# Third and fourth value groups by seven products of quarters, and another order of heads, linear attention and gates

## The chip, the cores and the metric

The kernel runs on one core of a Trainium2 chip as a single launch. The metric is the device time of a launch in microseconds (us), lower is better. Five engines work side by side: PE (TensorE, matrix products), ACT (ScalarE), DVE (VectorE), POOL (GpSimd) and SP (SyncE, which here only issues transfers from HBM). PE's weight loads are listed apart as PEld.

## The reference, cut to what matters

Two layers, each a mixer of three groups behind one input projection `w_in`, a gate on each group, one output projection and a layer norm. SEQ is 256 and D_MODEL is 2048.

```python
def hybrid_layer(x, mem, w_in, ...):
    h = x @ w_in
    a_q, a_k, a_v, a_z, b_q, b_k, b_v, b_z, b_lr, m_q, m_z = jnp.split(h, cuts, axis=-1)
    y_a = chunk_band_attention(a_q, a_k, a_v, rel_table)       # 8 heads of 128
    log_g = jax.nn.log_sigmoid(b_lr @ gate_w + gate_b) / GATE_TAU
    o_b = gla_chunk_recurrence(b_q, b_k, b_v, log_g)           # gated linear attention, 4 heads
    o_b = o_b * lax.rsqrt(jnp.mean(jnp.square(o_b), axis=-1, keepdims=True) + RMS_EPS) * gla_norm_g
    mk, mv = jnp.split(mem @ w_mem_kv, 2, axis=-1)
    y_m = memory_attention(m_q, mk, mv)                        # 4 heads of 128, 256 memory tokens
    y = concat([y_a * silu(a_z), o_b * silu(b_z), y_m * silu(m_z)])
    return layer_norm(DEEPNORM_ALPHA * x + y @ w_out, ln_g, ln_b)
```

## The kernel before

**Numbers.** Every large product is made of float32r operands split in two: a number is its rounded high part plus a low part, and a product takes three matmuls (high·high, low·high, high·low).

**The stream of weights.** All weights lie in one list, `loads`, in the order in which PE uses them. SP fetches each one into a tile `raw` of a ring of four (`RAWS`), ACT rounds it to the high part `wh` (ring of four), DVE subtracts to get the low part `wl` (ring of three). `take()` hands PE the next weight and calls `advance()`, which makes the casts of the weight three places ahead (`HI_AHEAD`), the subtraction two places ahead (`LO_AHEAD`) and starts the transfers for which the ring has room. PE and SP execute in the order of the program text (`manual_schedule`); on ACT and DVE a scheduler sets the order, in which weight work comes with high priority.

**Pieces.** One weight's matmuls are a piece. There are three kinds. A wide piece W (`ws_pieces`, 512 KB) has weights as the stationary side and x as the moving one: 16 matmuls, 8 of 512 and 8 of 256 columns. Its output comes transposed, as heads and gates need it. A piece O (`as_pieces` with 512 columns, 512 KB) has x stationary: 12 matmuls of 512. A value piece (`as_pieces` with 388 columns, 388 KB) is 12 matmuls of 388.

**Values.** `asv` holds the 1552 columns that are wanted with tokens on partitions: b_lr (16), b_v (512) and a_v (1024), as four groups of 388 (`w388[l, 0..3]`). Groups 0 and 1 together are a product of 256 tokens by 776 columns, which is cut into 2 x 2 blocks and done by seven block products (Strassen's method in Winograd's form) for each quarter of the 2048 rows: three products use a weight block as it lies in HBM (`plain_products`: quarters B11, B22, B21), four use sums of weight blocks (`sum_products`). A block product is a `quarter()`, 6 matmuls of 388 columns. The sums are made by DVE: B11 and B12, B22 are fetched into the tiles `term` (three of them, one set for all quarters), `high(d)` adds a second term to the first in place (L260) and ACT and DVE then split the sum. The x side has its differences in `diff`. Groups 2 and 3 are plain: two runs of eight value pieces, `values(2)` and `values(3)`, with `values` copying the result to `asv`.

**The order of work.** A layer runs: memory keys and values; linear attention's q and k (G_BQK); wide pieces of heads 0 to 3 (G_AQ0, G_AK0) and 4 to 7 (G_AQ1) mixed with the narrow quarters by the strings `PART_B` (a W between two plain products) and `PART_A` (a W between two sums); then, with no mixing, `values(2)`, the rest of the wide ones, `values(3)`, G_AK1, G_MQ, G_BZ, G_AZ0, G_AZ1, G_MZ: eight pieces each, 64 in all. After that the output projection.

**The generators.** Linear attention (`gla`), attention heads (`a_head`), memory heads (`m_head`) and the norm's work are Python generators that are stepped by `tick()` after each piece; `yield n` lets n pieces pass before the next step. They are what stands between pieces in PE's order, and they hide their work on ACT and DVE behind the pieces that pass meanwhile. Heads run two at a time from the list `waiting`; `finish(gens)` ticks, with no pieces in between, until they are done. In a head: scores on PE, bias and maximum on DVE, Exp on ACT, `yield 1`, scaling on DVE, `yield 3`, transposes on PE (L742), a copy on ACT (L744), `yield 2`, the product with the values on PE, a copy on ACT (L751). `gla` begins with an identity transpose of b_lr and the gate logits, builds its intra-chunk scores level by level, and ends with: products into PSUM, four copies to two tiles `sc` on ACT (L686), their squares (L693), an inverse root (`rsqrt`, L509 on ACT), scaling on DVE (L699), and then a wait for the gate z (`gate`), which `put_gate` makes out of the pieces G_BZ with a Silu on ACT (L1137); two multiplications by z on DVE (L705), `yield 2`, eight transposes on PE (L711).

**After the heads.** A gate's piece group (G_AZ0, G_AZ1, G_MZ) multiplies a group of heads `yraw[i]` by a Silu; `split_y` and `differences` prepare y for the output projection, which uses seven products of quarters too, for `QUARTERS` of its rows.

## Time and profile before

| | value |
|---|---|
| time, median of 3 runs (lowest to highest) | 910.93 us (910.86 to 911.02) |
| the profiled execution | 910.88 us |
| its span in the trace | 909.1 us |
| granted PE clock, mean over the span | 0.998 of full speed |
| PE busy | 902.0 us, 99% |
| PEld busy | 792.9 us, 87% |
| DVE busy | 715.9 us, 79% |
| ACT busy | 550.4 us, 61% |
| POOL busy | 9.0 us, 1% |
| moved by DMA | 196.20 MB, mean 216 GB/s |
| weight transfers of 512 KB into `raw` | 254, 4.3 us to landing |
| weight transfers of 388 KB into `raw` | 64, 3.6 us to landing |
| transfers of 388 KB into `term` | 24, 4.2 us to landing |

Read it so: the profiled execution is as long as the median run, and the span leaves 1.78 us of it outside of the trace. PE is busy nearly all of the span, so its idle time is small and DVE is the engine with the next highest load. Busy time on PE is modelled from pipelined matmuls, so the duration of a piece is best taken as the difference of two starts.

### The profile page before, as it was taken

Reading aid. Unit: us, or ns where it says so; the run is one execution under the profiler, and the core shown is the slowest. Engines: PE = TensorE matmul, PEld = TensorE weight load, DVE = VectorE, ACT = ScalarE, POOL = GpSimd, SP = SyncE. Lnnn points to the kernel's source line nnn. Section 1 sums busy time; section 2 is a strip of 40 time slices with the busy share of each in tenths; the row PEclk is TensorE's granted clock in tenths of the full one; section 3 lists DMA queues with packets and bytes.
Section 4 is the critical chain, followed back from the end, with each engine's and each line's share of the span. In section 5 each row is a group of like instructions: output and inputs, shape, how many; then the busy total and the mean of one; then the engine's idle time right before and its main releaser. Section 6 shows DMA issues by size and latency. Waiting matters only on the chain.

```text
span 909.1 us, 14442 instructions
## 1 busy us (share of the span) xinstructions
PE 902.0 (99%) x5437; PEld 792.9 (87%) x5437; DVE 715.9 (79%) x990; ACT 550.4 (61%) x803; POOL 9.0 (1%) x24
## 2 busy tenths in 40 slices
PE   9999999999999999999999999999999999999997
PEld 7889999998888888888888899999988888888885
DVE  5697788698764877799989667886886769778996
ACT  5675655576575775655569555556756657665551
POOL 1000000000000000000000000000000000000000
PEclk9999999999999999999999999999999999999999
DMA  8868786775545457876776687666654565669752
GB/s 301 289 202 281 262 273 200 241 256 181 156 154 168 143 166 255 257 251 213 242 221 199 193 292 252 226 195 185 216 178 141 179 205 167 252 208 302 249 191 93
DMA packets 66997, 196.20 MB, mean 216 GB/s; under 512 B 7024, under 2 KB 9840, under 8 KB 66928
## 3 DMA queue, kind: packets, MB, share of 16 engines
q1 hardware_dynamic: 66544, 195.18, 65.6%
q8 instruction: 42, 0.69, 0.3%
q14 instruction: 27, 0.22, 0.1%
q0 software_dynamic: 384, 0.11, 0.1%
HBM read 193.16 MB, written 2.10 MB: 215 GB/s over the span
## 4 chain that ended last, share of the span: by engine, by line
PE 99%; DMA 0%; ACT 0%; SPq 0%; ACTq 0%; issue 0%
PE ps L86 97%; PE ps L742 1%; DMA raw<-w 0%; PE ps L840 0%; PE ps L780 0%; PE ps L711 0%; ACT res L887 0%; PE ps L608 0%; PE ps L543 0%; ACT wh L362 0%; SPq L355 0%; ACTq L1299 0%; ACT row L880 0%; PE ps L878 0%; PE ps L864 0%
## 5 line engine op out<-in xcount | busy, mean ns | idle before, releaser
L268 DVE TENSOR_TENSOR wl<-raw,wh 128x1024 fp32r<-128x1024 f32 (+1 forms) x313 | 364.8, 1168 | 123.8 <-PE ps L86 83.5
L261 ACT CAST wh<-raw 128x1024 fp32r<-128x1024 f32 (+1 forms) x313 | 314.2, 1008 | 230.8 <-PE ps L86 135.5
L86 PE MATMUL ps<-x,wh 128*128 128x512 f32 x1280 | 404.2, 397 | 0.0
L86 PEld LDWEIGHTS ps<-x,wl 128*128 128x128 f32 x1280 | 240.4, 188 | 56.6
L86 PE MATMUL ps<-wh,x 128*128 128x512 f32 (+2 forms) x984 | 286.8, 373 | 1.0 <-ACT wh L362 1.0
L86 PE MATMUL ps<-x,wl 128*128 128x256 f32 x1280 | 252.2, 278 | 0.0
L86 PEld LDWEIGHTS ps<-x,wh 128*128 128x128 f32 x1280 | 199.7, 189 | 1.6 <-issue 0.3
L86 PEld LDWEIGHTS ps<-wh,x 128*128 128x128 f32 x984 | 179.1, 188 | 24.6 <-ACT wh L362 1.3
L86 PE MATMUL ps<-wl,x 128*128 128x512 f32 (+2 forms) x492 | 182.6, 371 | 0.0
L86 PEld LDWEIGHTS ps<-wl,x 128*128 128x128 f32 x492 | 92.4, 188 | 12.6 <-DVE wl L363 0.2
L261 ACT CAST wh<-term 128x776 fp32r<-128x776 f32 (+1 forms) x39 | 36.0, 924 | 50.5 <-DVE term L260 42.8
L268 DVE TENSOR_TENSOR wl<-term,wh 128x776 fp32r<-128x776 f32 (+1 forms) x39 | 41.5, 1065 | 14.0 <-PE ps L86 13.5
L260 DVE TENSOR_TENSOR term<-term,term 128x776 f32<-128x776 f32 (+1 forms) x39 | 41.3, 1060 | 0.5 <-DMA term<-w 0.5
L86 PE MATMUL ps<-wh,s 128*128 128x512 f32 (+1 forms) x144 | 41.2, 367 | 0.0
L86 PEld LDWEIGHTS ps<-wh,s 128*128 128x128 f32 x144 | 25.8, 188 | 3.2
L86 PE MATMUL ps<-wl,s 128*128 128x512 f32 (+1 forms) x72 | 26.5, 368 | 0.0
L733 ACT ACTIVATE sc<-sc,mx 128x128 f32<-128x128 f32 (+1 forms) x32 | 14.2, 444 | 8.2 <-DVE mx L731 8.2
L86 PE MATMUL ps<-wh,sc 128*128 128x388 f32 x64 | 16.5, 338 | 0.0
L86 PEld LDWEIGHTS ps<-wl,s 128*128 128x128 f32 x72 | 13.5, 188 | 1.6
L504 DVE TENSOR_TENSOR s<-raw,s 128x512 fp32r<-128x512 f32 (+1 forms) x23 | 12.6, 569 | 2.3 <-ACT s L503 2.3
L500 DVE SCALAR_TENSOR_TENSOR sz<-ps,sz 128x512 f32<-128x512 f32 x20 | 13.6, 686 | 0.9
L86 PE MATMUL ps<-w,x 128*128 128x512 f32 (+1 forms) x72 | 14.3, 356 | 0.0
(226 smaller groups left out, 701.7 us busy)
## 6 DMA issues: line engine op xcount, KB each, us to landing
raw<-w SPq DMA_DIRECT2D x254, 512.0 KB, 4.3
raw<-w SPq DMA_DIRECT2D x64, 388.0 KB, 3.6
term<-w SPq DMA_DIRECT2D x24, 388.0 KB, 4.2
term<-w SPq DMA_DIRECT2D x15, 512.0 KB, 4.7
bias<-relw SPq DMA_DIRECT2D x16, 192.0 KB, 3.8
res<-xT SPq DMA_DIRECT2D x4, 512.0 KB, 6.3
res<-xn SPq DMA_DIRECT2D x4, 512.0 KB, 5.0
raw<-memT SPq DMA_DIRECT2D x4, 512.0 KB, 4.8
```

The source lines that it names most:

```text
L86: pe.matmul(o, l, r, start=start, stop=stop, skip_group_check=True)
L260: in_order(dve.tensor_tensor(d.raw, d.raw, d.plus, op=ALU.add))
L261: act.copy(d.hi, d.raw)
L268: in_order(dve.tensor_tensor(d.lo, d.raw, d.hi.bitcast(F32), op=ALU.subtract))
L500: dve.scalar_tensor_tensor(dst, a, scale, dst, op0=ALU.mult, op1=ALU.add)
L504: dve.tensor_tensor(lo, src, hi.bitcast(F32), op=ALU.subtract)
L733: act.activation(s[:, own[t]], s[:, own[t]], AF.Exp, bias=mx[:, t:t + 1], accum_out=zs[:, t:t + 1])
L742: pe.transpose(ps[:, pt, i * P:(i + 1) * P], s[:, i * P:(i + 1) * P], ident)
```

## The change

Groups 2 and 3 of the values are done like groups 0 and 1. `PART_B` and `PART_A` become `PART_V`, one pair of patterns for each pair of groups: `B` is a plain product of a quarter, `T` a product with a sum, `W` a wide piece. G_AK1 joins the mixed stream, which has 36 W and 56 narrow pieces before all heads start, and 40 pieces are left: G_MQ, G_AZ0, G_BZ, G_MZ, G_AZ1, eight each. All heads and the linear attention run within these. `values()` is gone. Yields are shortened in `gla` and the heads, a list `scored` takes the place of `finish()` ahead of `differences` (they need a tile of q and k to be free, and a head that has its scores has read them), and heads 4 to 7 come behind the memory heads.

```diff
-PART_B = "WB" * 12
-PART_A = "TW" * 16
+PART_V = (("WB" * 4 + "WBB" * 4, "TWTWTTW" * 4), ("BBBW" * 4, "TWTWTTW" * 4))
...
-            stream = iter([Load(w512[l, g, p], (4, 256)) for g in (G_BQK, G_AQ0, G_AK0, G_AQ1) for p in range(8)][4:])
...
-            loads.extend(next(stream if c == "W" else plain) for c in PART_B)
-            add_sums(b11, b12, b21, b22, 388, PART_A, dict(W=stream))
-            group(w388[l, 2], 2, 388)
-            loads.extend(stream)
-            group(w388[l, 3], 2, 388)
-            for g in (G_AK1, G_MQ, G_BZ, G_AZ0, G_AZ1, G_MZ):
+            stream = iter([Load(w512[l, g, p], (4, 256)) for g in (G_BQK, G_AQ0, G_AK0, G_AQ1, G_AK1) for p in range(8)][4:])
+            sums = []
+            for v, (plains, added) in enumerate(PART_V):
+                b11, b12, b21, b22 = ([w388[l, v * 2 + n, 2 * q + k] for q in range(4)] for k, n in ((0, 0), (0, 1), (1, 0), (1, 1)))
+                plain = iter([Load(b, (2, 388)) for b in b11 + b22 + b21])
+                loads.extend(next(stream if c == "W" else plain) for c in plains)
+                add_sums(b11, b12, b21, b22, 388, added, dict(W=stream), sums)
+            for g in (G_MQ, G_AZ0, G_BZ, G_MZ, G_AZ1):
...
     gla:
-        yield 3
+        yield 2
         dve.scalar_tensor_tensor(xx, xx, 0.0, na, op0=ALU.min, op1=ALU.subtract)
...
         ready = [(gkf, gqf), decayed(dd)]
-        yield 3
+        yield 2
...
-                yield 1
+                if v == 0:
+                    yield 1
...
     a_head:
+        scored.append(h)
...
             dve.tensor_scalar(s[:, own[t]], s[:, own[t]], zs[:, t:t + 1], None, op0=ALU.mult)
-        yield 3
+        yield 2
...
-        yield 2
+        yield 1 if h < 4 else 2
         po, = yield from banks(1)
...
         release(po)
-        yield 1
...
-        values(2)
         add_heads(0)
-        run(wide)
-        values(3)
-        run(heads())
-        add_heads(1)
-        q = [hd.tile([P, 4, T], F32R, name=nm("mq"), tag="qk", bufs=4) for _ in range(2)]
+        mq = operand()
+        q = [mq[:, :, 0], mq[:, :, 1]]
...
         memory[:] = gens[-1]
+        add_heads(1)
...
-        run(as_pieces(xq[l], 512, put_gate, True))
         for i in range(1, 4):
             def gate(j, a, b):
...
-                if i == 1 and j == 0:
+                if i == 2 and j == 0:
                     finish(gens[0])
                     split_y(0, 0)
                     split_y(0, 2)
...
-                    finish(gens[min(i + 1, 3)])
+                    while len(scored) < (8 if q else 4):
+                        tick()
...
             run(ws_pieces(l, gate, cut_y if i == 3 else None))
+            if i == 1:
+                run(as_pieces(xq[l], 512, put_gate, True))
```

What the program's order becomes in layer 0 is shown at three places. The changed file has other line numbers than those of the profile: L683, L690, L505, L696, L702 and L708 there are L686, L693, L509, L699, L705 and L711 here, and L731, L740, L257, L264, L1130 are L733, L742, L261, L268, L1137.

The first place is the end of the linear attention, on ACT. The tiles `sc_2550` and `sc_2551` (before) are its result, `ms` the sums of its squares, `z` the gate, `sc_..,mx_..` the scores of a head. Before, in two pieces that lie apart in the row, the squares and the root, and then the gate:

```order
L693 ACTIVATE sq_2553,ms_2552<-sc_2550 128x128 x4
L261 CAST wh_2637<-raw_2451 128x1024
L693 ACTIVATE sq_2553,ms_2552<-sc_2551 128x128 x4
L261 CAST wh_2664<-raw_2532 128x1024
L509 ACT_TABLE_LOAD
L509 ACTIVATE rs_u_416_2628<-ms_2552,eps 128x8
```

```order
L261 CAST wh_2917<-raw_2857 128x1024
L261 CAST wh_2941<-raw_2875 128x1024
L751 COPY yr_1683<-ps 128x256 x2
L261 CAST wh_2963<-raw_2903 128x1024
L1137 ACT_TABLE_LOAD
L1137 ACTIVATE z_2959<-ps 128x1024
```

After, on the same engine (the linear attention's result is now `sc_3130` and `sc_3131`, and heads 4 and 5 are `sc_3225` and `sc_3237`):

```order
L690 ACTIVATE sq_3133,ms_3132<-sc_3131 128x128
L505 ACT_TABLE_LOAD
L505 ACTIVATE rs_u_515_3212<-ms_3132,eps 128x8
L731 ACT_TABLE_LOAD
L731 ACTIVATE sc_3225,zs_3228<-sc_3225,mx_3227 128x128
L731 ACTIVATE sc_3225,zs_3228<-sc_3225,mx_3227 128x256
L731 ACTIVATE sc_3237,zs_3240<-sc_3237,mx_3239 128x128
L731 ACTIVATE sc_3237,zs_3240<-sc_3237,mx_3239 128x256
L257 CAST wh_3273<-raw_3116 128x1024
L1130 ACT_TABLE_LOAD
L1130 ACTIVATE z_3263<-ps 128x1024
L257 CAST wh_3295<-raw_3196 128x1024
```

Root, the Exps of two heads and the Silu of the gate have moved together, with three table loads; before, 27 rows lay between the root and the gate's table load.

The second place is what PE has there: the transposes of the linear attention's result. Before, they stand alone between two wide pieces:

```order
L86 MATMUL ps<-x_478,wh_2917 128x512 x2
L86 MATMUL ps<-x_478,wl_2943 128x256 x2
L711 MATMUL ps<-ident,sc_2550 128x128 x4
L711 MATMUL ps<-ident,sc_2551 128x128 x4
L86 MATMUL ps<-x_530,wh_2941 128x512 x2
```

After, the transposes of heads 4 and 5 stand right behind them:

```order
L86 MATMUL ps<-x_478,wh_3192 128x512 x2
L86 MATMUL ps<-x_478,wl_3247 128x256 x2
L708 MATMUL ps<-ident,sc_3130 128x128 x4
L708 MATMUL ps<-ident,sc_3131 128x128 x4
L740 MATMUL ps<-ident,sc_3225 128x128 x3
L740 MATMUL ps<-ident,sc_3237 128x128 x3
L86 MATMUL ps<-x_530,wh_3245 128x512 x2
```

Between the last products of the linear attention (`st,qb`) and these transposes there are now four pieces, the values' products of two memory heads and the scores of heads 4 and 5; before there were 16 pieces, with the transposes and products of heads 4 and 5, all of heads 6 and 7 and the scores of two memory heads.

The third place is SP's row of transfers where plain products are mixed with wide pieces. Before (128x776 is a 388 KB weight, 128x1024 one of 512 KB):

```order
L238 DMA raw_620<-w 128x1024
L238 DMA raw_626<-w 128x776
L238 DMA raw_664<-w 128x1024
L238 DMA raw_686<-w 128x776
L238 DMA raw_698<-w 128x1024
```

After, in the plain products of groups 2 and 3:

```order
L234 DMA raw_1362<-w 128x776
L234 DMA raw_1395<-w 128x776
L234 DMA raw_1428<-w 128x776
L234 DMA raw_1450<-w 128x1024
L234 DMA raw_1462<-w 128x776
L234 DMA raw_1480<-w 128x776
L234 DMA raw_1504<-w 128x776
L234 DMA raw_1516<-w 128x1024
```

Three narrow transfers now stand ahead of each wide one, in a ring of four.

More of the change, by code (lines that the diff above doesn't have):

```diff
@@ L166, in add_sums @@
                     loads.append(d)
-            def group(g, kp, n):
-                loads.extend(Load(g[i], (kp, n)) for i in range(16 // kp))
             for p in range(8):
@@ L1026, in hybrid_trunk_kernel @@
         asv = per.tile([P, 2, 1552], F32, name=nm("asv"), tag="asv")
-        bias = {}
-        def values(i):
-            run(as_pieces(xq[l], 388, lambda acc: act.copy(asv[:, :, i * 388:(i + 1) * 388], acc)))
+        bias, scored = {}, []
         def put_gla(i, a, b):
@@ L1041, in stream @@
             yield from ws_pieces(l, put_gla, None, 4)
-            for _ in range(3):
+            for _ in range(4):
                 yield from heads()
@@ L1115, in hybrid_trunk_kernel @@
             beside(others)
[L1116 removed]
+        gens.append([m_head(h, q, mk, mv, yraw[2][:, h]) for h in range(4)])
         waiting.extend(gens[-1])
         memory[:] = gens[-1]
+        add_heads(1)
         yq, ydiff = [], []
```

71 lines of the change are left out of this document (35 added, 36 removed).

## The prediction

> **What bounds the kernel now.** I read the page first (engines, chain), then PE's timeline in the mixed stage for the length of a piece, then groups by form for ACT and DVE, then the timelines at the two places where the new order lays small work close together. The page's rows of busy time, its chain, and three of its transfer rows:
>
> ```profile
> PE 902.0 (99%) x5437; PEld 792.9 (87%) x5437; DVE 715.9 (79%) x990; ACT 550.4 (61%) x803; POOL 9.0 (1%) x24
> ...
> PE 99%; DMA 0%; ACT 0%; SPq 0%; ACTq 0%; issue 0%
> ...
> raw<-w SPq DMA_DIRECT2D x254, 512.0 KB, 4.3
> raw<-w SPq DMA_DIRECT2D x64, 388.0 KB, 3.6
> term<-w SPq DMA_DIRECT2D x24, 388.0 KB, 4.2
> ```
>
> The chain is PE for 99%: nothing else is late now, so a removed matmul is worth its whole time, and every wait that the new order makes is paid in full. The execution took 910.88 us (span 909.1 and 1.78 around it), 0.05 under the median, so the sum is made against 910.9. A change under 0.2%, 1.8 us, is about what a measurement of this kernel can't tell from none.
>
> **What is removed.** PE's timeline in the mixed stage (start, us, ...):
>
> ```profile
> 100.16 0.62 PE L86 MATMUL ps<-x,wh 128*128 128x512 f32 x2
> ...
> 102.95 0.52 PE L86 MATMUL ps<-wh,x 128*128 128x388 f32 x2
> 103.30 0.34 PE L86 MATMUL ps<-wl,x 128*128 128x388 f32 x1
> 103.48 0.52 PE L86 MATMUL ps<-wh,x 128*128 128x388 f32 x2
> 103.83 0.34 PE L86 MATMUL ps<-wl,x 128*128 128x388 f32 x1
> 104.01 0.62 PE L86 MATMUL ps<-x,wh 128*128 128x512 f32 x2
> ```
>
> From 100.16 to 102.95 is a wide piece, 2.79 us; from 102.95 to 104.01 a quarter of six matmuls, 1.06, or 0.177 each. Groups 2 and 3 take 2 x 8 x 12 = 192 matmuls of 388 a layer, and 7 x 4 x 6 = 168 by quarters: 24 less a layer, 48 in all, 48 x 0.177 = **8.5 us**. Wide pieces are the same in number.
>
> **What is added off PE.** For each layer twelve more transfers into `term` (9.5 MB in all beside 196), 12 more adds into terms and 4 into `raw`, and 12 more casts and subtractions. Their prices, with those of a 512 KB weight, from the groups by form (xcount | busy, mean ns):
>
> ```profile
> L268 DVE TENSOR_TENSOR wl<-raw,wh 128x1024 fp32r<-128x1024 f32 x249 | 303.7, 1221 | 91.1 <-PE ps L86 59.7 <-issue 12.4 <-ACT wh L261 9.0
> L268 DVE TENSOR_TENSOR wl<-term,wh 128x776 fp32r<-128x776 f32 x24 | 23.2, 967 | 11.9 <-PE ps L86 11.7
> L260 DVE TENSOR_TENSOR term<-term,term 128x776 f32<-128x776 f32 x24 | 23.0, 959 | 0.0
> L261 ACT CAST wh<-raw 128x1024 fp32r<-128x1024 f32 x249 | 260.8, 1051 | 186.0 <-PE ps L86 115.2 <-DMA raw<-w 41.4 <-issue 13.9
> ```
>
> On DVE that is 32 adds by 0.96 and 24 subtractions by 0.97, 54 us, and 12 combinations more; 716 becomes some 780 of 910. It lies beside PE's products. In a row `TWTWTTW`, PE has 4 x 1.06 + 3 x 2.79 = 12.6 us of work and DVE 4 x (0.96 + 0.97) + 3 x 1.22 = 11.4 at most. These two windows show that DVE can be this full (columns: window, length, PE, PEld, DVE, ACT, POOL, clock, DMA share, GB/s), the second with the cover nearly gone:
>
> ```profile
> 109.40:171.50 62.10, 62.10 (x357) 56.52 (x356) 51.84 (x59) 31.87 (x37) 0.00 (x0) 1.00 0.72 232
> 366.80:455.40 88.60, 88.60 (x392) 73.23 (x391) 81.43 (x83) 50.21 (x51) 0.00 (x0) 1.00 0.74 243
> ```
>
> PE lost nothing with DVE at 92%. I cost it at nothing. Four more table loads on ACT count only at the two places below.
>
> **The ring.** In `BBBW` a wide weight always meets the same one of four `raw` tiles. That tile's cycle is landing 4.3, cast 1.05, subtraction 1.22 and some 0.2 to issue (my estimate from the gaps between these rows), 6.8 us; PE needs 3 x 1.06 + 2.79 = 5.97 for the four pieces. Four rounds lose at most 4 x 0.8 = 3.3 us, out of a stock of three weights cast ahead, which is worth three narrow pieces (3.2) or more. The nearest stage of before, one narrow to one wide with the first terms:
>
> ```profile
> 84.00:98.00 14.00, 14.00 (x82) 12.73 (x81) 7.99 (x8) 7.12 (x9) 0.00 (x0) 1.00 0.85 297
> ```
>
> 297 GB/s without a wait of PE; `BBBW` asks (3 x 0.397 + 0.524 MB) / 5.97 us = 288. Between no loss and 3.3 us a layer I take 0.3, near the row without a loss: **0.6 us**.
>
> **Heads 0 and 1.** The gates' logits, and behind them the copies of the heads' transposes, are rows of one queue on ACT. Before, the same work (first a row of PE, last the copies' mean from the groups):
>
> ```profile
> 256.13 0.82 PE L742 MATMUL ps<-ident,sc 128*128 128x128 f32 x6
> ...
> 176.88 0.83 ACT L554 ACTIVATE sc<-ps,gb 128x256 f32<-128x256 f32 x2
> ...
> 179.28 0.63 ACT L558 ACTIVATE sc<-sc 128x512 f32<-128x512 f32 x1
> 179.92 1.28 ACT L559 ACT_TABLE_LOAD   x1
> 181.22 0.63 ACT L559 ACTIVATE sc<-sc 128x512 f32<-128x512 f32 x1
> ...
> L744 ACT COPY sc<-ps 128x384 f32<-128x384 f32 x16 | 6.8, 478 | 0.0
> ```
>
> From the end of the logits' products, PE has a wide piece, the six transposes (0.82, of which the modelled end overlaps the next row; some 0.6) and another wide piece before it wants the first copy: 2.79 + 0.6 + 2.79 = 6.2. In the new order a weight's cast and a scaling of 512 columns (0.63, as L558) come on ACT ahead of L559's table load, and that cast's `wh` is free only when the first wide piece ends, at 2.79: 2.79 + 1.05 + 0.63 + 1.30 + 0.63 + 0.48 = 6.9 for the first copy, 7.4 for the second, which is wanted at 6.6. At the least, with the cast free at once, there is no wait (the same sum begins 1.3 earlier, behind L554 and DVE's L557); at the most 0.8. I take 0.7 a layer, since the ring of `wh` is full in this stage: **1.4 us**.
>
> **The end of the linear attention.** This is the main cost. PE's rows there, before:
>
> ```profile
> 241.45 1.58 PE L86 MATMUL ps<-qk,qk 128*128 128x128 f32 x8
> 242.68 0.58 PE L86 MATMUL ps<-x,wh 128*128 128x512 f32 x1
> ...
> 247.64 0.74 PE L86 MATMUL ps<-x,wh 128*128 128x512 f32 x2
> ...
> 311.58 1.53 PE L86 MATMUL ps<-sc,mv 128*128 128x256 f32 x12
> 312.96 0.63 PE L86 MATMUL ps<-x,wh 128*128 128x512 f32 x2
> ```
>
> Count from the end of `st,qb` (247.64 before). In the new order PE has two memory heads' products (312.96 - 311.58 = 1.38), two heads' scores (242.68 - 241.45 = 1.23) and four pieces (11.16): it wants the transposes at 13.8. ACT and DVE, before:
>
> ```profile
> 247.31 2.39 ACT L686 COPY sc<-ps 64x512 f32<-64x512 f32 x4
> ...
> 254.02 1.04 ACT L261 CAST wh<-raw 128x1024 fp32r<-128x1024 f32 x1
> 255.08 1.28 ACT L509 ACT_TABLE_LOAD   x1
> 256.37 0.30 ACT L509 ACTIVATE rs_u<-ms,eps 128x8 f32<-128x8 f32 x1
> 259.21 1.29 DVE L699 TENSOR_TENSOR sc<-sc,rr 128x512 f32<-128x512 f32 x2
> 292.70 1.28 ACT L1137 ACT_TABLE_LOAD   x1
> 294.00 1.03 ACT L1137 ACTIVATE z<-ps 128x1024 f32<-128x1024 f32 x1
> ...
> L733 ACT ACTIVATE sc<-sc,mx 128x128 f32<-128x128 f32 (+1 forms) x32 | 14.2, 444 | 8.2 <-DVE mx L731 8.2
> L751 ACT COPY yr<-ps 128x256 f32<-128x256 f32 x16 | 5.7, 367 | 1.3 <-PE ps L86 1.3
> ```
>
> The first copy starts at -0.3. From it to the table load were 255.08 - 247.31 = 7.77 with two casts; now one cast less and two copies of 0.37 more, 7.5. Then in ACT's row: load and root 1.6, load 1.3, four Exps 4 x 0.44 = 1.8, cast 1.04, load 1.3, Silu 1.03. z is there at -0.3 + 7.5 + 8.1 = 15.2. DVE multiplies the first half by it (1.29 / 2 = 0.65), subtracts a weight (1.22), multiplies the second half (0.65): 17.7. PE has done the first four transposes in the meantime and stands from 14.3 to 17.7: 3.4 us a layer, **6.8 us**. Before, the same transposes came 47 us after the copies and waited for nothing. What could shorten it: nothing on ACT in that row can start earlier than the one ahead of it, but squares that overlap a little, and a subtraction that falls in another gap, could take 0.5 to 1.2; what could lengthen it is a late cast.
>
> The Trainium skill ("ScalarE: Activation LUTs", section "What ACT_TABLE_LOAD costs") puts a switch of tables at about 2.7 us with the drain of the engine. The rows show otherwise: the cast ends at 255.06, the load starts at 255.08 and the root at 256.37, 1.3 us in all.
>
> **The sum.** 910.9 - 8.5 + 0.6 + 1.4 + 6.8 = 911.2. Taking 0.2 a layer off the end's wait, for the overlaps just named, I say **910.8**: no change that can be told.
>
> **The rivals.**
> *The waits are half or less (faster).* For it: every wait is a difference of two long sums; if ACT's row at the end runs 1.7 us shorter and the head's copies come in time, 910.8 - 3.4 - 1.4 = 906.0, and with no waits at all 902.4. Against it: the order of ACT is fixed, and its rows have measured lengths. Center 905.5.
> *The ring (slower).* If landing in `BBBW` is 4.3 or more throughout and the stock gives only 1 us, each layer loses 2.3: 910.8 - 0.6 + 4.6 = 914.8. It decides from a landing above 5.97 - 1.05 - 1.22 - 0.2 = 3.5 us for 512 KB. For it: the median is 4.3; the first terms of the next sums go out in the same stage. Against: 297 GB/s without a wait.
> *PE's clock (slower).* These rows show what the clock does (the clock stands ahead of the DMA share):
>
> ```profile
> 903.00:905.00 2.00, 1.13 (x6) 0.64 (x4) 1.11 (x2) 1.67 (x4) 0.00 (x0) 1.00 0.52 188
> 905.00:907.00 2.00, 0.00 (x0) 0.00 (x0) 0.00 (x0) 0.01 (x1) 0.00 (x0) 0.58 0.92 330
> ```
>
> With PE idle for 2 us the granted clock is 0.58, with gaps 1.00. If the piece behind the long wait ran at 0.58, it would take 2.79 / 0.58 = 4.8, 2.0 more a layer: 914.8. The Trainium skill ("TensorE: Matmul & The Clock Gate", "Part 1: The HAM clock gate") has the clock halve after an idle window of 3.4 us that runs freely; by that rule a wait of this length would seldom fill a window, and these rows neither show nor exclude it.
> *Loads twice as dear (slower).* If a load held ACT for two times 1.28 where functions alternate, the three at the end add 3.8 a layer: 918.5. No row speaks for it.
>
> **How the numbers follow.** No change by the sum 0.44, waits half or less 0.31, ring 0.16, clock 0.07, loads 0.02. The first case's own range is 908.3 to 913.3, and it gives 0.07 to faster, 0.32 to no change, 0.05 to slower. So faster 0.38, the same 0.32, slower 0.30. The range 904.5 to 914.8 leaves out the lower part of the second case, half of the third and fourth and the last.
>
> **What would show it.** In the changed trace: 48 fewer matmuls of 388 on PE; a gap of about 3.4 us in PE ahead of the transposes L708, with the multiplication L702 named as its releaser, twice; about 0.6 us ahead of the first product with values; PE without gaps in `BBBW`. I am wrong if z's Silu ends well before 15 us after `st,qb`, if gaps with a `raw` transfer as their releaser come up among the narrow pieces, or if DVE's subtractions are late in the forty pieces.

## The result, and the profile after

The changed kernel takes 937.62 us (937.25 to 937.87) against 910.89 us of the kernel before beside it: 1.0294 times as long (95% interval 1.0276 to 1.0312). It is 26.7 us slower; 910.8 was forecast, in a range up to 914.8. With the 8.5 us of matmuls that are gone, 35 us of waits are to be found. In one of the runs below, that of the banks' order, one execution of four took 2425.81 us; it is left out of that run's time.

The page of the changed kernel, its engines, its chain and its weight transfers:

```profile
span 935.6 us, 14558 instructions
...
PE 905.8 (97%) x5389; PEld 785.5 (84%) x5389; DVE 769.6 (82%) x1058; ACT 573.2 (61%) x833; POOL 8.9 (1%) x24
...
PE 80%; DVE 8%; DMA 5%; ACT 4%; issue 3%; SPq 0%; ACTq 0%; DVEq 0%
...
raw<-w SPq DMA_DIRECT2D x254, 512.0 KB, 4.5
raw<-w SPq DMA_DIRECT2D x64, 388.0 KB, 4.3
term<-w SPq DMA_DIRECT2D x48, 388.0 KB, 4.1
```

The 48 matmuls are gone (5437 to 5389). The chain, 99% PE before, has 20% of other engines, and a value weight now lands in 4.3 us, not 3.6.

Where it went, by windows (window, length, PE, PEld, DVE, ACT, POOL, clock, DMA share, GB/s). Each goes from a layer's first value product to the first product with a sum in its output projection. Before:

```profile
64.41:373.63 309.22, 309.22 (x2033) 278.17 (x2032) 233.94 (x342) 193.32 (x302) 3.23 (x7) 1.00 0.65 211
511.72:819.40 307.68, 307.68 (x2026) 276.83 (x2025) 234.00 (x336) 190.65 (x293) 1.62 (x4) 1.00 0.64 208
```

After, each of the two in two parts, the mixed stream and the forty pieces (with the first pieces of the output):

```profile
64.06:230.84 166.78, 162.74 (x914) 146.23 (x913) 138.63 (x158) 91.86 (x112) 0.00 (x0) 1.00 0.74 253
230.84:382.80 151.96, 146.89 (x1098) 126.92 (x1096) 122.16 (x219) 112.39 (x205) 3.22 (x7) 1.00 0.55 182
521.38:684.51 163.13, 160.89 (x914) 146.72 (x913) 133.44 (x144) 90.39 (x108) 0.64 (x2) 1.00 0.76 255
684.51:845.31 160.80, 148.44 (x1091) 127.45 (x1088) 127.41 (x227) 111.66 (x201) 0.98 (x2) 0.99 0.53 170
```

Layer 0 takes 318.74, 9.5 more than before, layer 1 323.93, 16.3 more: together 25.8 of the 26.7. Since 4.25 us of matmuls are gone in each, layer 0 has 13.8 us of waits and layer 1 has 20.5. A stream is 36 x 2.79 + 56 x 1.06 = 159.8 us of pieces: 7.0 us of the waits of layer 0 lie there and 3.3 of layer 1. The forty pieces have the rest, 6.8 and 17.2. (PE busy is modelled; the differences of starts show more waits than the idle time.)

**In the stream.** The stage `BBBW`, in layer 0 and 1:

```profile
153.00:177.00 24.00, 21.75 (x120) 18.95 (x119) 16.03 (x19) 12.82 (x17) 0.00 (x0) 1.00 0.87 294
606.00:630.00 24.00, 21.76 (x120) 19.21 (x119) 16.19 (x18) 13.13 (x17) 0.00 (x0) 1.00 0.86 289
```

PE is without work for 2.2 us in each, 3.4 and 3.3 by the starts of its matmuls, while DVE is busy for two thirds and ACT for half: a weight is late. By the starts, nearly all of it falls into the third of the four rounds, which takes 9.28 us in both layers; the others take 5.97 to 6.06. What SP issued from 155 to 162 us landed late, and from 159 on the DMA engines had no time left:

```profile
raw<-w SPq DMA_DIRECT2D x4, 388.0 KB, 6.8
term<-w SPq DMA_DIRECT2D x3, 388.0 KB, 6.6
raw<-w SPq DMA_DIRECT2D x1, 512.0 KB, 6.8
...
159.00:162.00 3.00, 3.00 (x19) 2.53 (x18) 1.91 (x2) 0.91 (x2) 0.00 (x0) 1.00 1.02 347
162.00:165.00 3.00, 2.12 (x12) 1.57 (x10) 0.49 (x1) 1.23 (x2) 0.00 (x0) 1.00 1.01 393
```

The three terms in between, 1.2 MB, are those of the first sums. Layer 0 loses 3.4 more from 85 to 110 us, in the first plain products. In the stages of the sums, where DVE has most to do, PE waits for nothing:

```profile
177.00:230.80 53.80, 53.80 (x310) 49.13 (x309) 47.89 (x53) 29.55 (x34) 0.00 (x0) 1.00 0.70 242
630.00:684.50 54.50, 54.50 (x314) 49.74 (x313) 48.67 (x54) 29.87 (x36) 0.64 (x2) 1.00 0.71 242
```

**At the first transposes.** PE's and DVE's rows (start, us; in brackets the idle time before and what ended it):

```profile
230.84 0.38 PE L539 MATMUL ps<-ident,asv 128*16 128x128 f32 x2
232.19 0.55 DVE L471 TENSOR_TENSOR asv<-asv,ps 128x388 f32<-128x388 f32 x1
232.84 0.30 PE L860 MATMUL ps<-ident,lng 128*128 128x128 f32 x1 [1.61 <-issue]
```

The next matmul begins when DVE's last combination, L471, has read its PSUM bank: 1.8 us here, 1.7 in layer 1.

**At the end of the linear attention.** ACT, DVE and PE:

```profile
326.26 1.28 ACT L1130 ACT_TABLE_LOAD   x1
327.56 1.03 ACT L1130 ACTIVATE z<-ps 128x1024 f32<-128x1024 f32 x1
...
328.62 0.69 DVE L702 TENSOR_TENSOR sc<-sc,z 128x512 f32<-128x512 f32 x1 [0.41 <-ACT z L1130]
329.23 1.22 DVE L264 TENSOR_TENSOR wl<-raw,wh 128x1024 fp32r<-128x1024 f32 x1
330.36 0.69 DVE L702 TENSOR_TENSOR sc<-sc,z 128x512 f32<-128x512 f32 x1
...
329.37 0.66 PE L708 MATMUL ps<-ident,sc 128*128 128x128 f32 x4 [0.60 <-DVE sc L702]
331.20 0.63 PE L708 MATMUL ps<-ident,sc 128*128 128x128 f32 x4 [1.17 <-DVE sc L702]
```

2.1 us by the starts, and the same in layer 1.

**In layer 1 alone.** DVE and PE:

```profile
719.33 2.08 DVE L855 TENSOR_TENSOR res<-res,sc 128x512 f32<-128x512 f32 x3 [2.35 <-DMA sc<-ln_g]
...
725.42 1.69 PE L86 MATMUL ps<-mk,x 128*128 128x256 f32 x12 [1.64 <-DVE pairs L636]
...
758.16 0.69 PE L86 MATMUL ps<-sc,sc 64*64 64x64 f32 x32 [3.26 <-DVE sc L583]
...
815.33 1.07 PE L740 MATMUL ps<-ident,sc 128*128 128x128 f32 x6 [2.13 <-DVE sc L735]
```

Three waits for DVE that layer 0 has not or has shorter. L855 is the norm of the residual (`norm_residual`), sixteen operations of 0.69 us that run only in layer 1, among the forty pieces. DVE also stands still for the rows that they multiply by, 9.2 us in four places:

```profile
DVE res L855 <- DMA sc<-ln_g: 9.2, 4, 3.6
```

**The clock.** Three windows of 5 us, the first with PE idle for 3 us:

```profile
755.00:760.00 5.00, 1.84 (x37) 1.60 (x38) 5.00 (x13) 4.97 (x13) 0.00 (x0) 1.00 0.51 183
770.00:775.00 5.00, 3.34 (x56) 2.41 (x54) 4.23 (x11) 3.06 (x5) 0.00 (x0) 0.87 0.17 66
775.00:780.00 5.00, 5.00 (x24) 4.44 (x24) 2.02 (x4) 2.82 (x15) 0.00 (x0) 0.79 0.47 144
```

The clock falls in the linear attention's last products, where the matmuls are small and PE is without work for 1.6 us in all: 5 x 0.13 + 5 x 0.21 = 1.7 us lost. Behind the longest wait (758) it does not. The trace has the clock at half from 773.73 to 777.15 us, for 3.41 us. Windows of that length on the same grid, two around the wait that ends at 758, the one ahead of the halved one, and it:

```profile
753.25:756.67 3.42, 1.65 (x37) 1.08 (x35) 3.42 (x7) 3.39 (x6) 0.00 (x0) 1.00 0.46 148
756.67:760.08 3.41, 1.92 (x38) 1.64 (x39) 3.41 (x10) 3.38 (x11) 0.00 (x0) 1.00 0.43 159
770.32:773.73 3.41, 1.79 (x39) 1.31 (x42) 3.31 (x9) 1.52 (x3) 0.00 (x0) 1.00 0.16 61
773.73:777.15 3.42, 3.42 (x31) 3.09 (x24) 2.91 (x5) 1.58 (x5) 0.00 (x0) 0.50 0.43 114
```

The wait of 3.3 us lies across the border of two windows and leaves PE about half busy in each; the small matmuls and their waits lie in one, which is half busy too. The last section counts what follows such windows.

### The profile page after: what moved, and what is told of

Its sections match the earlier page's. It is cut to its first block, busy times and chain, and to the rows that moved or that the text cites. A ratio compares the mean times of both kernels' runs of the same rounds, so it can differ in the third digit from the quotient of the medians.

```text
span 935.6 us, 14558 instructions
## 1 busy us (share of the span) xinstructions
PE 905.8 (97%) x5389; PEld 785.5 (84%) x5389; DVE 769.6 (82%) x1058; ACT 573.2 (61%) x833; POOL 8.9 (1%) x24
## 4 chain that ended last, share of the span: by engine, by line
PE 80%; DVE 8%; DMA 5%; ACT 4%; issue 3%; SPq 0%; ACTq 0%; DVEq 0%
PE ps L86 78%; DVE wl L264 4%; DMA raw<-w 2%; DMA sc<-ln_g 1%; ACT wh L257 1%; DMA sc<-ln_b 1%; PE ps L740 0%; DMA lm<-lmask 0%; DVE res L855 0%; DVE mx L763 0%; PE ps L836 0%; DVE sc L583 0%; DVE sc L582 0%; DVE sc L574 0%; ACT sc L731 0%
## 5 line engine op out<-in xcount | busy, mean ns | idle before, releaser
L264 DVE TENSOR_TENSOR wl<-raw,wh 128x1024 fp32r<-128x1024 f32 (+1 forms) x313 | 364.5, 1169 | 94.3 <-PE ps L86 44.9
L257 ACT CAST wh<-raw 128x1024 fp32r<-128x1024 f32 (+1 forms) x313 | 313.0, 1007 | 203.7 <-PE ps L86 91.9
L86 PE MATMUL ps<-wh,x 128*128 128x512 f32 (+2 forms) x824 | 245.5, 379 | 0.0
L86 PEld LDWEIGHTS ps<-wh,x 128*128 128x128 f32 x824 | 150.4, 188 | 24.2 <-ACT wh L358 0.4
L86 PE MATMUL ps<-wl,x 128*128 128x512 f32 (+2 forms) x412 | 155.7, 378 | 0.0
L257 ACT CAST wh<-term 128x776 fp32r<-128x776 f32 (+1 forms) x63 | 56.3, 893 | 81.2 <-DVE term L256 64.8
L264 DVE TENSOR_TENSOR wl<-term,wh 128x776 fp32r<-128x776 f32 (+1 forms) x63 | 64.6, 1026 | 7.6 <-PE ps L86 6.8
L256 DVE TENSOR_TENSOR term<-term,term 128x776 f32<-128x776 f32 (+1 forms) x63 | 64.5, 1023 | 6.7 <-DMA term<-w 6.4
L86 PE MATMUL ps<-wh,s 128*128 128x388 f32 (+1 forms) x208 | 58.3, 362 | 1.8 <-ACT wh L257 1.8
L86 PE MATMUL ps<-wl,s 128*128 128x388 f32 (+1 forms) x104 | 37.9, 364 | 0.8 <-DVE wl L264 0.8
L86 PE MATMUL ps<-wl,sc 128*128 128x388 f32 x64 | 21.7, 339 | 0.3 <-DVE wl L264 0.3
L86 PEld LDWEIGHTS ps<-wh,sc 128*128 128x128 f32 x128 | 21.5, 189 | 0.0
L256 DVE TENSOR_TENSOR raw<-raw,term 128x776 f32<-128x776 f32 (+1 forms) x21 | 21.4, 1021 | 0.0
L855 DVE TENSOR_TENSOR res<-res,sc 128x512 f32<-128x512 f32 x16 | 10.6, 689 | 9.7 <-DMA sc<-ln_g 9.2
```

What stands on the lines that cost most here:

```text
L86: pe.matmul(o, l, r, start=start, stop=stop, skip_group_check=True)
L256: in_order(dve.tensor_tensor(d.raw, d.raw, d.plus, op=ALU.add))
L257: act.copy(d.hi, d.raw)
L264: in_order(dve.tensor_tensor(d.lo, d.raw, d.hi.bitcast(F32), op=ALU.subtract))
L855: dve.tensor_tensor(r, r, row, op=op)
```

## The experiments

The diffs are against the changed kernel if nothing else is said. Times are medians; the kernel before took 910.86 to 911.24 beside all of them.

**The order alone.** Groups 2 and 3 are plain pieces again, in the stream.

```diff
-("BBBW" * 4, "TWTWTTW" * 4))
+("BW" * 16, ""))
...
+        def values():
+            for i in (2, 3):
+                yield from as_pieces(xq[l], 388, lambda acc: act.copy(asv[:, :, i * 388:(i + 1) * 388], acc), at=i * 2)
...
-            narrow = plain_products(l, asv, n1, n2)
+            narrow = plain_products(l, asv, n1, n2) if v == 0 else values()
```

> Groups 2 and 3 as plain value pieces (16 of 12 matmuls, one wide piece behind each), all else as in the changed kernel: the new order alone. 8.5 us of matmuls come back. The trace of the changed kernel has some 13.5 us of PE waits in the mixed stream (layer 0: 3.3 in the first plain products, 3.4 in the second ones, 1.8 at the first transposes; layer 1: 3.3 and 1.7) and some 21 in the forty pieces. Theory 'both': the stream's waits go, but for those of the first plain products, and the forty pieces' stay: 937.6 + 8.5 - 10.2 = 936. Theory 'products' (the whole loss comes with the seven products): about 911. Theory 'order' (the whole loss is the forty pieces'): 937.6 + 8.5 = 946.

943.45 us, ratio 1.0356 (1.0340 to 1.0371). With the new order alone the kernel loses 32.4 us; with the products it loses 5.8 less, their 8.5 and what this run has of waits of its own, less the waits that they make. The gap at the first transposes is not there (0.2 us from one start to the next): without products there are no combinations. The forty pieces' waits are all there. My 936 was too low: I had counted on the stream's waits to go, and 2.6 us a layer of others came in `BWBW` (for DVE's combinations of the first pair of groups, by the rows that ended them), and 5.1 us of halved clock against 1.7. Without the two (5.2 and 3.4 us), 24 us remain to the order.

**The sums' terms later.**

```diff
-                ahead = FIRST_SUM_AHEAD if
+                ahead = 5 if d.sum[0] == 4 else FIRST_SUM_AHEAD if
```

> The first terms of groups 2 and 3 are fetched five weights ahead and not ten, so that they don't go out in the middle of the plain products BBBW. If it is their 1.2 MB in one go that makes the ring's transfers land in 7 us there, the 3.3 us a layer of waits go: 937.6 - 6.7 = 931. If the ring of four itself is too short for three narrow weights to one wide one, the waits stay: 937 to 938. If the terms now come too late for the first sum, it gets slower: 938 to 942.

939.36 us (1.0294 to 1.0325). The waits of the stage are 3.0 and 2.8 us by the starts, where they were 3.4 and 3.3. But the terms have not left the stage: in layer 0 they are issued from 162.1 to 166.5 us and not from 155.5 to 158.0, and the slow round is now the fourth (8.50 us; the third has 6.46). The DMA engines are full there, and not before:

```profile
159.00:162.00 3.00, 3.00 (x19) 2.65 (x18) 2.07 (x3) 1.56 (x2) 0.00 (x0) 1.00 0.86 250
168.00:171.00 3.00, 2.82 (x16) 2.40 (x15) 0.97 (x1) 1.33 (x3) 0.00 (x0) 1.00 1.00 388
171.00:174.00 3.00, 2.05 (x8) 1.31 (x8) 2.46 (x3) 2.06 (x3) 0.00 (x0) 1.00 0.99 381
```

In layer 1 it is the same, 8.12 us in the fourth round. The waits went where the terms went; a run with the terms outside of the stage was not made.

**Five raw tiles.** The room is that of the biases, which now lie in the third term's tile.

```diff
-HI_AHEAD, LO_AHEAD, RAWS = 3, 2, 4
+HI_AHEAD, LO_AHEAD, RAWS = 3, 2, 5
...
-            bias[h] = hd.tile([P, 384], F32, name=nm("bias"), tag="bias", bufs=3)
+            bias[h] = pairs_of_bias[:, h % 2, :384]
```

> Five raw tiles in place of four; the room comes from the biases of the heads, which now lie two at a time in the third term's tile and are fetched when the score before has read its own. If the ring is too short for BBBW (a tile's cycle of 6.8 us and more, four tiles, one weight each 1.7 us, where PE takes one each 1.49), the waits of 3.3 us a layer go, and with them part of those of layer 0's first plain products: 937.6 - 6.7 to 10 = 928 to 931. If the DMA engines are what is short there, they stay: 936 to 938. Biases that come late would cost 0 to 2 us, in the forty pieces.

934.97 us (1.0228 to 1.0271). The same two windows:

```profile
153.00:177.00 24.00, 22.69 (x127) 20.27 (x126) 17.34 (x18) 14.34 (x18) 0.00 (x0) 1.00 0.77 269
606.00:630.00 24.00, 23.54 (x133) 21.28 (x133) 18.43 (x19) 14.45 (x19) 0.00 (x0) 1.00 0.80 278
```

PE idles 1.3 and 0.5 us there, for 2.2 and 2.2, and by the starts the waits of the stage fall from 6.7 to 3.1 and those of layer 0's first plain products from 3.4 to 1.1. So a longer ring takes away half of the stage's waits and most of the others (the first plain products wait for 0.4 to 1.1 us in all four profiles with five tiles). It does not clear the DMA engines: their mean share is lower (0.77 and 0.80), but in layer 0 they are full again from 156 to 162 us (1.00 and 1.01), behind the terms, and the waits that are left follow at once. The terms make the transfers late, and the ring's length sets how much of that PE feels. The total won 2.6 of these 5.9 us, for this profile lost 6.8 us to the halved clock and the changed kernel's 1.7.

**Two wide pieces to three narrow ones.**

```diff
-("BBBW" * 4, "TWTWTTW" * 4))
+("BWBBW" * 4, "TWTWTT" * 4))
```

> The plain products of groups 2 and 3 as BWBBW and the sums as TWTWTT: four wide pieces a layer go from the sums to the plain products, three narrow weights to two wide ones instead of three to one. The ring waits 3.3 us a layer in BBBW; fetching the terms later did not change this. If the stage is short of time for its transfers (the DMA engines are busy 0.87 of it, the highest share of any), they go, 937.6 - 6.7, and the sums pay where VectorE has 4 x 1.76 + 2 x 1.13 = 9.3 us of work to 9.8 of PE: 0 to 2 us a layer. So 931 to 935. If the waits have another reason: 937 to 942.

948.85 us (1.0402 to 1.0433), outside of all that was expected. `BWBBW` waits for 0.3 us at most, which a short ring and a shortage of transfer time would both have, but the sums now wait: 3.4 and 4.0 us among the last rows of them and 3.5 at the first transposes, in each layer. Rows of the sums with 9.8 us of PE for 9.3 of DVE are too tight. Besides, this profile loses 10.2 us to the halved clock.

**The combinations' priority, their banks, the sums' adds, and one piece more.** Four edits on the gap at the first transposes (shortened, and in part in words):

```diff
 e5:  c12, c21, c22 = asv[:, 0, n2], asv[:, 1, n1], asv[:, 1, n2]
+     with tc.high_priority(AHEAD) around the six combinations
 e11:
-            if d.plus is not None:
+            if d.plus is not None and (d.shape[1] == 512 or d.sum[0] < 4):
 e16: the heads and the linear attention are added behind the first piece of G_MQ
+        queries = ws_pieces(l, put_mq)
+        run(queries, 1)
+        beside(gens[0] + others)
+        add_heads(0)
+        run(queries)
 e18:
-        free[:] = [4, 5, 6, 7]
+        free[:] = [6, 7, 4, 5]
```

> The combinations of the third and fourth group's products (L466 to L471) get the high priority on VectorE that weight work has. The first PE work after the stream (the scores of heads 0 and 1) writes the four PSUM banks that these combinations read, and in the changed kernel it begins 1.8 us late in each layer, when the last combination ends. If this is the reason, both gaps go and nothing else: 937.6 - 3.5 = 934. If weights are then late by the 3.3 us of combinations, it is given back: 937 to 938.

> Leaves out the sums of the weights for groups 2 and 3 (sixteen adds of 0.96 us on VectorE a layer; the casts and subtractions stay). If VectorE's arrears at the end of the sums make the gap of 1.8 us at the first transposes, where a higher priority of the combinations changed nothing, both gaps go: 937.6 - 3.5 = 934. If they come from the order of the last piece alone: 937 to 938.

> Linear attention and heads start one wide piece later, so that two pieces (5.6 us more one: 8.4) and not 5.6 us lie between the last sum and the first work on the combinations' PSUM banks; VectorE has 7.6 us of combinations, subtractions and a total there. If that sum is the reason for the gaps of 1.8 us at the first transposes: -3.5, 934; the forty pieces have one piece less behind, which may cost up to 2.8 at the end of the heads. If it is a wait for something else, the gaps stay: 937 to 940.

> One line: after the stream the free PSUM banks are given out in the order 6, 7, 4, 5. The combinations read 6 and 7 first and 5 last; the first transposes and scores now take 6 and 7. If the gap of 1.8 us a layer at the first transposes is the wait for the bank that the last combination reads, most of it goes: 937.6 - 2.5 to 3.5 = 934 to 935. If VectorE's row itself is what the heads wait for (their scores' scaling stands behind the combinations), the wait moves to the transposes of heads 0 and 1: 937 to 938.

The priority: 937.57 us (1.0277 to 1.0307), the gaps as before, 1.8 and 1.7. Without the adds: 939.35 us (1.0293 to 1.0326), the gaps as before; DVE even stood idle for 1.8 us ahead of the last subtractions, so it isn't in arrears. One piece later: the gaps are gone, and the time is 945.24 us (1.0357 to 1.0396). The banks: the gap is 1.0 in layer 0 and gone in layer 1, and the time is 939.60 us (1.0301 to 1.0342). So the gap is the wait for the bank that the last combination reads, on account of what DVE has to do behind the last sum, and it stands in no relation to DVE's load before. That neither cure makes the kernel faster has two reasons that the profiles show. One piece later, the wait at the linear attention's end is 6.7 us a layer, with a piece of its cover gone:

```profile
801.69 1.94 PE L708 MATMUL ps<-ident,sc 128*128 128x128 f32 x8 [6.50 <-DVE sc L702]
803.42 1.49 PE L740 MATMUL ps<-ident,sc 128*128 128x128 f32 x6
804.56 1.20 PE L86 MATMUL ps<-x,wh 128*128 128x512 f32 x2
805.56 0.63 PE L86 MATMUL ps<-x,wl 128*128 128x256 f32 x2
```

And behind such a wait PE runs at half its clock: a pair of matmuls of 512 columns took 1.20 us, where 0.63 is usual. Windows of 5 us there:

```profile
795.00:800.00 5.00, 0.19 (x2) 0.00 (x0) 4.03 (x13) 3.70 (x10) 0.00 (x0) 0.98 0.20 59
800.00:805.00 5.00, 3.31 (x15) 3.34 (x16) 3.44 (x5) 2.02 (x4) 0.00 (x0) 0.50 0.87 215
805.00:810.00 5.00, 5.00 (x25) 4.28 (x25) 4.42 (x9) 2.44 (x7) 0.11 (x1) 0.84 0.61 251
```

0.1 + 2.5 + 0.8 = 3.4 us lost; over the whole profile 10.2, and in that of the banks' order 5.1.

**The mask later.** The two operations that wait for a transfer go behind the sums.

```diff
-                dve.tensor_copy(lmask, lm)
-                dve.tensor_tensor(eye, ident[:, :CH], ident[:, CH:], op=ALU.add)
             for c in added:
                 run(wide if c == "W" else narrow, 1)
+            if l == v == 0:
+                dve.tensor_copy(lmask, lm)
+                dve.tensor_tensor(eye, ident[:, :CH], ident[:, CH:], op=ALU.add)
```

> In layer 0, VectorE's two operations on the transferred mask and identity (L1064, L1065) stand behind the sums of the first groups instead of ahead of them. In the trace VectorE stands 1.2 us for these transfers, and PE has 3.3 us of gaps from 85 to 110 us, which layer 1 doesn't have. If the standing makes those behind 98 us: 937.6 - 2 to 2.4 = 935.4. If it is the x differences that share this stage: 937 to 938.

939.06 us (1.0291 to 1.0321). The waits from 85 to 110 us are 2.3 and not 3.4 us. That shows nothing of the mask: in the other profiles with four tiles, which all leave it in its place, the same waits are 1.8 to 3.9 us, and with the rows fetched ahead, an edit of layer 1, they are 2.2. In the total a gain of that size can't be told, where this profile lost 6.8 us to the clock.

**The residual's norm: rows fetched ahead, left out, left out before, in other places.**

```diff
 e3:
+            for row, a in zip(fetched, (ln_g, ln_b)):
+                sp.dma_start(row, a[l:l + 1, columns(n)].to_broadcast([P, 512]))
+            yield 4
 e4, e12 (of the kernel before):
-            others = [norm_residual(l - 1)]
+            others = [iter([1])]
 e10:
                 run(as_pieces(xq[l], 512, put_gate, True))
+                if l:
+                    beside(others)
 e15:
         for c in OUT_B[l]:
             run(sequences[c], 1)
+        finish([arrears])
```

> The norm's gain and offset rows of layer 1 (L852) are fetched four pieces before VectorE multiplies by them, and not just ahead. In the trace VectorE stands 9.2 us for these transfers in layer 1's forty pieces with the weights' and the heads' work queued behind. If this standing makes layer 1's waits there (some 15 us against 5.5 in layer 0), most of the difference goes: 937.6 - 7 to 9.5 = 928 to 931. If it is the sixteen multiplications themselves (11 us of VectorE), little goes: 936 to 938.

> Leaves out the normalisation of the residual in layer 1 (sixteen VectorE operations and eight transfers). If these are why layer 1 waits longer than layer 0 in its forty pieces: 937.6 - 10 = 927.6. If layer 1 waits for another reason: 936 to 938. The difference to the kernel with the rows fetched ahead is the price of the operations themselves.

> The kernel before, with the normalisation of the residual left out in layer 1 as above. If its place among 64 pieces covered it wholly: 910.9, no change. If it cost there too: 905 to 909, and the loss by the new order is smaller than 8.6 by that.

> The normalisation of the residual in layer 1 starts behind G_BZ, in the last sixteen pieces, with yields of 3 for 6; nothing is left out. Leaving it out took 8.6 us off. If it is only in the wrong place, all of that comes: 929. If its sixteen operations need the cover of the whole stage, wherever they stand, it waits in the gates instead: 934 to 938.

> The residual's norm of layer 1 in the first ten pieces of the output projection, behind all heads and gates, with yields of 2. Nothing is left out. If only the forty pieces lack cover for it, it is as good as leaving it out: 929. If VectorE and the fetch of its rows delay the output's weights: 931 to 936.

Rows ahead: 938.18 us (1.0287 to 1.0322), nothing won. But the edit did not do what it was for. The rows land when they did (719.22 us the first, for 719.31), DVE's operations begin as they land, and DVE stands for them almost as long, 8.0 us for 9.2:

```profile
DVE res L857 <- DMA sc<-ln_g: 8.0, 4, 3.6
```

So this run does not say what the standing costs. Left out: 929.04 us (1.0186 to 1.0224), 8.6 us. Left out of the kernel before: 911.25 us, ratio 1.0001 (0.9992 to 1.0011). So sixteen operations, with the fetch of their rows, cost nothing among 64 pieces and 8.6 us among forty; this is the largest single part of the loss. How much of it is the operations' time and how much the standing stays open. Behind G_BZ: 934.02 us (1.0230 to 1.0260), the earlier waits gone and a wait of 3.1 us at heads 6 and 7 in their place. In the output projection: 934.45 us (1.0240 to 1.0271); there the weights' subtractions are late, 5.7 us from 838 to 862. No place in the new order that was tried covers it.

**The linear attention's last transposes a piece later.**

```diff
             dve.tensor_tensor(on[par], on[par], z[:, par], op=ALU.mult)
-        yield 2
+        yield 3
```

> The transposes at the end of the linear attention come one piece later (yield 3 for yield 2), behind those of heads 4 and 5. They waited 2.1 us a layer for the multiplication by the gate. A piece more covers 2.79: 937.6 - 4.2 = 933.4. If the heads' transposes then wait in their place, since their Exps and scalings stand in the same row of ScalarE and VectorE, half or less is won: 935.5 to 937.6.

940.48 us (1.0298 to 1.0333). In layer 0 the wait is gone (2.1 to 0). In layer 1 it is gone too, but heads 6 and 7 wait 5.8 us where they waited 2.3, behind the norm's operations, and 6.8 us are lost to the clock.

**Together.** First the norm behind G_BZ (e10), five tiles (e13) and the later transposes (e7); then e15, e16, e13 and e7; then the banks' order (e18), e13, e7 and the norm over the last eight pieces and the first eight of the output:

```diff
 e19:
+            if l and i == 3:
+                beside(others)
             run(ws_pieces(l, gate, cut_y if i == 3 else None))
...
 norm_residual:
-            yield 6
+            yield 4
```

> Three mendings together: the residual's norm behind G_BZ (alone -3.6), five raw tiles (alone -2.6), the linear attention's last transposes a piece later (alone +2.9, since in layer 1 the wait moved to heads 6 and 7 behind the norm's operations). If the parts add: 934. If the mended tail gains once the norm is out of its way (2.1 us a layer): 927 to 929. If waits only move from one place of the forty pieces to another: 933 to 937.

> e15 and e16 with five raw tiles and the later transposes. If the waits found are independent: 937.6 - 8.6 (norm) - 6 (ring) - 3.5 (first transposes) - 4.2 (last transposes) = 915. If part of what is won comes back as waits at the next place or as a halved clock behind the waits that remain: 919 to 926.

> The banks' order, five raw tiles, the last transposes a piece later, and the residual's norm in the last eight pieces and the first eight of the output projection (yields of 4). From e14 (924.4): its last large waits, 5.9 us of PE at the transposes of heads 6 and 7 in layer 1 and 3.4 us of halved clock behind them, are the norm's and go, and so do the first transposes' 3.5; some 1 to 3 us come back in the output. 924.4 - 9.3 - 3.5 + 2 = 914 if the causes named are all there is; 918 to 924 if waits take each other's place.

924.43 (1.0136 to 1.0171), 925.60 (1.0145 to 1.0175) and 923.12 us (1.0114 to 1.0155). Half of the loss is mended, more than the parts alone had given (13.2 us in the first, where its parts gave 2.6 + 3.6 - 2.9 = 3.3), as a wait that is taken away alone often comes up at the next place. (The halved clock has a share in it: 6.8 us each in the profiles of five tiles and of the later transposes, 3.4 in that of the first three together.) None reaches the kernel before. In the last of them the largest waits are behind the norm's operations in the last gate and the output projection, 6.5 us in all and 1.7 of halved clock with them:

```profile
841.66 0.79 PE L86 MATMUL ps<-wl,s 128*128 128x512 f32 x1 [2.12 <-DVE wl L264]
845.73 0.50 PE L86 MATMUL ps<-wl,x 128*128 128x512 f32 x1 [1.14 <-DVE wl L264]
```

## Why the prediction was wrong

*The matmuls, 8.5 us.* Right: 48 fewer, each at 0.177.

*Heads 0 and 1, 0.7 a layer.* Right: 0.5 us, in both layers, in all of these profiles but those in which the heads begin a piece later.

*The end of the linear attention, 3.2 a layer.* The mechanism was right and the size was off by a third. z was to be there 15.2 us after `st,qb`; the last product of it began at 313.49 and the Silu ended at 327.56 + 1.03 = 328.59, 15.1 later. But PE, which was to be there after 13.8, came 1.0 us late itself, for the two memory heads ahead of it waited: 2.1 us of wait and not 3.2.

*The ring, 0.3 a layer.* This step failed: 3.4 and 3.3 us, and 3.4 us more in layer 0's first plain products (`WB` and `WBB`), where nothing was forecast. I set 297 GB/s of an alternating stage beside the 288 that `BBBW` asks (by its own terms 287) and took the value near "no loss". But alternating, PE takes two weights in 3.85 us, one in 1.9, and in `BBBW` four in 5.97, one in 1.5. The figure that was wrong is the landing, 4.3 us: with the terms of the next sums on the way it was 6.8. With that the step's own sum, an estimate, is 6.8 + 1.05 + 1.22 + 0.2 = 9.3 us for the tile of the wide weight, and the slow round took 9.28. That the total met the upper end of 3.3 is luck: it was to be four rounds of 0.8 and came as one of 3.3, and the rounds with earlier landings lost nothing. I had named the terms for the ring's rival, and gave it a chance of 0.16. Two runs speak to it: with the terms later the wait moves along, with five tiles half of it goes. The 3.4 us of the first plain products fall to 1.1 with five tiles; what makes weights late there stays open.

*The sums on VectorE, nothing.* Right where it was argued, in the stages of sums: DVE was busy 47.89 of 53.80 us and PE waited for nothing. The step failed at the end of the sums, where the last six combinations hold the four PSUM banks that the heads need at once (3.5 us). Before, the plain groups stood between; I looked at what the change adds and not at what used to lie behind the last sum.

*What had no term at all: the residual's norm.* The sum treated layer 1 as a second layer 0. It is the only one with these sixteen operations (11 us of DVE), and they cost 8.6 us. This is the step whose failure cost most: the sum put at nothing, without a reason, what the shorter cover does to work that the change leaves alone. A window of the kernel before would have warned, that of layer 0's 64 pieces:

```profile
171.50:366.80 195.30, 195.30 (x1391) 174.99 (x1389) 142.47 (x237) 129.04 (x224) 3.23 (x7) 1.00 0.59 190
```

DVE was free for 53 of 195 us. Forty pieces have sixteen value pieces (twelve matmuls of 0.177, 2.1 us) and eight wide ones less, 56 us of time, and of DVE only their subtractions, 16 x 0.97 + 8 x 1.22 = 25 us: 22 us stay free in layer 0 and 11 in layer 1, by this estimate, for work that comes in chains, and in layer 1 DVE stands 9.2 us for rows. The waits go the same way: 6.8 us in layer 0's forty pieces and 17.2 in layer 1's, of which 8.6 are the norm's by the run without it and 1.7 the clock's. A term for cover lost, stage by stage and layer by layer, was missing, beside the three places that I priced.

*The rivals.* The ring's waits came true, at more than the 2.3 us a layer that it gave. The clock came true in part: 1.7 us and not 4.0 in this profile, and not behind the wait ahead of L708, for which the rival was made. Its 0.58 was no clock either: the trace of the kernel before has the clock at 1.00 up to 905.31 us and at 0.50 from there, and 0.58 is the mean of a window with both. With the Trainium skill's rule ("TensorE: Matmul & The Clock Gate", "Part 1: The HAM clock gate") half the clock is granted after an idle window of 3.4 us that runs freely, and comes back after a busy one. The traces agree with half (0.50 in 800:805) and with the length: the losses of all these profiles are 0, 1.7, 3.4, 5.1, 6.8 and 10.2 us, multiples of 3.4 us at half speed. They do not agree with idle: the window from 770.32 to 773.73 had PE busy for 1.79 of 3.41 us, and half the clock came behind it.

What adds up, in us by starts and medians: `BBBW` 6.7 and the first plain products 3.4, first transposes 3.5, heads 0 and 1 1.0, the linear attention's end 4.2, the norm 8.6, clock 1.7: 29.1 of 35. The other 6 are small waits (0.2 to 0.8 each) in both layers' forty pieces, and stay without a cause of their own: that each would go with more pieces between the steps was not tried.

## What to carry to other kernels

When work that has no part in the change is pressed into fewer covering pieces, sum each engine's work against the cover for every stage and every layer, with the work that only one layer has; pricing the places that the order shows side by side is not enough. A ring of buffers is priced by items per time: compare a tile's cycle with the time in which the consumer takes as many items as the ring has tiles, round by round, with the landing of the round in which other transfers go out and not with the median. When a run is to take a cause away, see in its trace that it did: the terms fetched later were still in the stage, and the rows fetched ahead landed no earlier. A wait mended alone tends to come up again at the next place: judge the parts by the waits in the profile, and the whole by a run with all of them.

## What the runs showed of the hardware that I had not expected

A wait on PE can cost nearly twice its length: in several profiles a gap of 2 to 7 us was followed by 3.4 us at a granted clock of 0.5 (pairs of matmuls of 1.20 us for 0.63), 1.7 us more for each time. What decides is not the wait but how busy PE is, by the profile's modelled times, in the one window of 3.41 us ahead. The halved stretches of a profile start whole windows apart (46 from 773.73 to 930.75 us in the changed kernel's). Counted on this grid over all twenty profiles, for windows at full clock and without the last 15 us of each kernel: 33 windows had PE busy for less than 0.48, and half the clock followed each of them; of 24 between 0.48 and 0.53 it followed 6, and of 5140 above that none. So a wait of 3.3 us across a border can pass, and waits of 1.6 us in all among small matmuls can cost 1.7 us. Where the grid lies differs from run to run, and this may be why times spread: the kernel without the norm took 932.43 us in the run with a mean clock of 0.994 and 928.43 to 929.48 in those of 0.997 to 0.999. With five raw tiles the two do not go together so well (932.54 and 935.98 us, both at 0.993), so this is not shown.
